# A refitted order of steps, five large probability tiles for four, and other makers of low parts in a hybrid attention layer

## The chip, the cores and the metric

The kernel runs on one core of one Trainium2 chip, all of its work in one launch. The metric is the device time of an execution in microseconds (us). Before the change the median of three timed runs is 360.08 us (359.06 to 360.17). A core has five engines with a queue each, all run in the order in which they were issued: PE (TensorE, with its weight loads as PEld), DVE (VectorE), ACT (ScalarE), POOL (GpSimd) and SP (SyncE, here only DMA issues).

## The reference, cut to what matters

One layer on 512 tokens of width 1024, all in float32:

```python
h = x @ w_in                      # 1024 -> 4114 columns: q, k, v, gates of three mixers
o_nsa = nsa_mixer(...)            # 6 heads: compressed, selected and window attention, gated
o_sb  = stick_breaking_mixer(...) # 4 heads: log_sigmoid scores, reversed cumsum, exp, times v
o_hg  = hgrn2_mixer(...)          # 6 heads: gated linear attention in chunks of 64
mixed = concat([o_nsa * silu(nsa_z), o_sb * silu(sb_z), rms(o_hg) * silu(hg_z)])
x = layer_norm(ALPHA * x + mixed @ w_out, ln_g, ln_b)
```

## The kernel before, in words

Precision first, since it sets the amount of work. A float32 matrix product is made of products of a high and a low part: `hi` is the operand rounded to the narrower type fp32r, `lo` is what is left, and three matmuls (hi with hi, lo with hi, hi with lo) add up in PSUM. So each piece of weights that arrives in a `raw` tile needs two more instructions before PE can use it: the cast to `hi` and the making of `lo`. `load_part` (L277 to L293) does this for 128x1024 elements at a time. The table `SPLITS` says, for each group's first and for its later parts, who makes `lo`: 3 means that ACT casts (L281) and negates (L282), and a DMA of POOL's queue adds the original onto the negation (L284 reads the weights from DRAM again if the group is in `FROM_DRAM`, L286 reads `raw`); 1 means a subtraction on DVE, 0 the same subtraction on POOL (both L293).

The work is cut into named steps. Projections with weights as the moving operand (`blocks`, matmuls L337, 512 columns) are hf1, hq, sq, sk, q, q_kc, vc_ks, kw_sz, sz_nz and nz; with tokens as rows (`tiles`, L353, 256 columns) hi, hi_sv, sv_vs, vw and hz. p0, p1 and p2 are the pairs of heads of the gated linear attention: six times DVE makes a masked query `qz` (L821) and a key `kz` (L796, exponential on ACT), PE multiplies them (L823), DVE copies the product under a mask into `att` (L831); after that come `kt`, the state `st` and the output. s0 to s3 are the stick-breaking heads (scores on PE L385, then ACT and DVE by turns, DVE's running sum L703); v0 to v3 multiply their probabilities with values: `pv` transposes them into `mb` (L403), ACT casts `ph` and DVE makes `pl` (L183, L184), PE adds into the one accumulator `pc` (L410), and `fold` (ACT L140, DVE L425) empties it into `su`. ck and cv are the compressions (L551), c0, c1 and n0 to n11 the scores and probabilities of the first mixer (probabilities in large tiles `pt` of 128x1280 from the pool p5), w0 to w11 their products with values in the way of v0 to v3. f, m, o0, o1 and end finish: `end` multiplies the rest with w_out (L912), adds and normalises.

The order is written out by hand. `ORDER` is a list of step names; a step that has been started is a generator, and each further mention runs it to its next yield. Every mention issues its instructions on all engines at that place; the tile framework then sets each engine's queue from that, with the parts under `high_priority` ahead. So moving a name in `ORDER` moves instructions on PE, DVE, ACT, POOL and SP together. `BUFS` sets the number of buffers of each pool: there is one accumulator (psc=1), so a step v or w can start adding only when the one before has been folded.

Of the kernel before, what the change touches and what calls it, by code (L numbers as in the profile page):

```python
# [38 lines left out]
    hf1=((OFF["hf"] + 256, 128), (OFF["hq"], 128)),  # L39
    hq=((OFF["hq"] + 128, 256),),  # L40
    hi=((OFF["hi"], 256),),
    hi_sv=((OFF["hi"] + 256, 128), (OFF["sv"], 128)),
    sq=((OFF["sq"], 256),),
    sk=((OFF["sk"], 256),),
    sv_vs=((OFF["sv"] + 128, 128), (OFF["vs"], 128)),
    q=((OFF["q"], 64), (OFF["q"] + 192, 64), (OFF["q"] + 64, 64), (OFF["q"] + 256, 64)),
    q_kc=((OFF["q"] + 128, 64), (OFF["q"] + 320, 192)),
    vc_ks=((OFF["vc"], 256),),
    kw_sz=((OFF["kw"], 128), (OFF["sz"], 128)),
    vw_g_hz=((OFF["vw"], 146), (OFF["hz"], 128)),  # L50
    hz=((OFF["hz"] + 128, 256),),
    sz_nz=((OFF["sz"] + 128, 128), (OFF["nz"], 128)),
    nz=((OFF["nz"] + 128, 256),),
)

ORDER = (
# [7 lines left out]
    "end "  # L64
)

BUFS = dict(at=3, g2=31, kkp=4, ma=2, mb=4, nb=3, p0=1, p5=4, psa=3, psc=1, raw=3, sa=8, sb=6, ta=8, tb=10, ti=1,
    w=16)

SPLITS = dict(ck=(1, 1), cv=(1, 1), hf1=(1, 1), hi=(3, 0), hi_sv=(0, 1), hq=(1, 0), hz=(1, 0), kw_sz=(0, 0),  # L70
    nz=(1, 1), o0=(0, 3), o2=(1, 1), o3=(3, 3), sk=(3, 1), sq=(3, 1), sv_vs=(3, 1), sz_nz=(3, 1), vc_ks=(1, 1),
    vw_g_hz=(3, 1))

FROM_DRAM = ('sq', 'sk', 'q', 'q_kc', 'o0', 'o2', 'o4', 'o6')
# [50 lines left out]
class Net:  # L125
# [826 lines left out]
    def body(self, ctx):  # L952
        tc, nc, a = self.tc, self.nc, self.a

        def pool(name, **k):
            n = BUFS.get(name, 1)
            if n:
                k["bufs"] = n
            return ctx.enter_context(tc.tile_pool(name=name, **k))
# [287 lines left out]
```

## Time and profile before

| | |
|---|---|
| median of three runs | 360.08 us |
| profiled execution | 359.79 us |
| its span, first to last instruction | 357.8 us |
| mean granted TensorE clock | 0.994 of full speed |
| busy: PE, DVE, ACT, POOL | 339.3, 291.3, 239.0, 82.4 us |

The span is what the trace shows; 2.0 us of the execution's time lie outside it. A row of the timeline gives the start, the time from there to the end of the last instruction of the row, and in brackets the idle time of the engine ahead of it with what ended that. Busy time is no measure of what bounds the kernel at one place: for that the idle time of PE is looked at stretch by stretch.

### The profile page before, as it was taken

The page shows a single profiled execution, that of the slowest core. Times are in us where ns is not written, and L with a number is a line of the kernel's source. Part 1 is how long each engine was busy: PE and PEld are TensorE (multiplying, and loading weights), DVE is VectorE, ACT ScalarE, POOL GpSimd, SP SyncE. Part 2 cuts the span into 40 slices and gives each one's busy share as a digit, 9 for nine tenths or more (in the row PEclk, how much of TensorE's full clock was granted, in tenths as well). Part 3 has the DMA queues.
Part 4 walks back from the last instruction along what each step waited for, and adds up shares of the span by engine and source line. Part 5 has one row for each costly group of instructions (what it writes and reads, how often), then busy time and mean ns, then how long its engine had stood idle before and what let it go on. Part 6 is the DMA issues. An engine that isn't in the chain of part 4 may idle for free.

```text
span 357.8 us, 5876 instructions
## 1 busy us (share of the span) xinstructions
PE 339.3 (95%) x1994; PEld 288.9 (81%) x1994; DVE 291.3 (81%) x671; ACT 239.0 (67%) x535; POOL 82.4 (23%) x131
## 2 busy tenths in 40 slices
PE   7999999999989989999999999899999999999990
PEld 6778999978778878777887998778888888788880
DVE  4569899889899999987897767668989875769785
ACT  4586772525669997757576666699787874697260
POOL 5063460000400210102400033142021201410074
PEclk9999999999999999999999999999999999999997
DMA  7765547230335564030327847291432180080014
GB/s 267 277 199 159 152 119 236 72 104 2 63 115 117 120 148 87 2 118 2 106 79 203 278 168 205 67 208 34 135 67 52 42 202 23 29 196 12 0 60 176
DMA packets 15909, 42.07 MB, mean 118 GB/s; under 512 B 2626, under 2 KB 3138, under 8 KB 15880
## 3 DMA queue, kind: packets, MB, share of 16 engines
q1 hardware_dynamic: 13432, 33.42, 28.4%
q0 software_dynamic: 2448, 8.29, 13.0%
q8 instruction: 16, 0.26, 0.3%
q14 instruction: 13, 0.11, 0.1%
HBM read 37.06 MB, written 2.12 MB: 110 GB/s over the span
## 4 chain that ended last, share of the span: by engine, by line
PE 62%; DVE 19%; ACT 8%; issue 4%; DMA 3%; POOL 1%; SPq 0%; DVEq 0%; ACTq 0%; POOLq 0%
PE pi L337 20%; PE pi L912 11%; PE pi L353 10%; PE pc L410 6%; PE mb L403 4%; PE ma L385 4%; PE ma L823 3%; DVE sr L703 3%; DMA raw<-w_in 2%; DVE ct L511 2%; DVE qz L821 1%; DVE att L831 1%; DMA xt<-xt 1%; DVE sz L704 1%; POOL ho L447 1%
## 5 line engine op out<-in xcount | busy, mean ns | idle before, releaser
L337 PE MATMUL pi<-xh,hi 128*128 128x512 f32 x160 | 47.4, 406 | 0.1
L337 PE MATMUL pi<-xl,hi 128*128 128x512 f32 x160 | 46.2, 396 | 0.0
L337 PE MATMUL pi<-xh,lo 128*128 128x512 f32 x160 | 46.1, 396 | 0.0
L912 PE MATMUL pi<-hi,mx 128*128 128x512 f32 (+1 forms) x134 | 43.0, 391 | 0.0
L337 PEld LDWEIGHTS pi<-xh,lo 128*128 128x128 f32 x160 | 29.4, 188 | 5.9 <-DVE lo L293 0.4
L337 PEld LDWEIGHTS pi<-xl,hi 128*128 128x128 f32 x160 | 29.5, 188 | 5.7
L337 PEld LDWEIGHTS pi<-xh,hi 128*128 128x128 f32 x160 | 28.5, 188 | 5.5 <-ACT hi L291 0.6
L184 DVE TENSOR_TENSOR pl<-mb,ph 128x384 fp32r<-128x384 f32 (+1 forms) x48 | 27.8, 593 | 3.4 <-ACT ph L183 2.5
L291 ACT CAST hi<-raw 128x1024 fp32r<-128x1024 f32 (+3 forms) x24 | 23.5, 983 | 9.4 <-PE pi L337 4.9
L649 DVE CUSTOM_DVE_ANT_0 pt<-ma,nb 128x256 f32<-128x256 f32 (+3 forms) x42 | 21.3, 513 | 9.5 <-PE ma L385 9.0
L651 ACT ACTIVATE pt<-pt,mn 128x256 f32<-128x256 f32 (+3 forms) x42 | 24.5, 583 | 6.4 <-DVE mn L649 5.9
L183 ACT CAST ph<-mb 128x384 fp32r<-128x384 f32 (+1 forms) x48 | 23.2, 514 | 7.6 <-PE mb L403 7.4
L912 PEld LDWEIGHTS pi<-hi,mx 128*128 128x128 f32 x134 | 24.3, 188 | 4.4 <-PE pi L337 0.4
L353 PE MATMUL pi<-hi,xh 128*128 128x256 f32 (+1 forms) x160 | 27.4, 287 | 0.0
L353 PE MATMUL pi<-hi,xl 128*128 128x256 f32 (+1 forms) x160 | 27.2, 285 | 0.0
L353 PE MATMUL pi<-lo,xh 128*128 128x256 f32 (+1 forms) x160 | 26.7, 285 | 0.0
L912 PE MATMUL pi<-lo,mx 128*128 128x512 f32 (+1 forms) x67 | 26.1, 390 | 0.0
L353 PEld LDWEIGHTS pi<-hi,xh 128*128 128x128 f32 x160 | 23.0, 191 | 0.7
L353 PEld LDWEIGHTS pi<-hi,xl 128*128 128x128 f32 x160 | 22.7, 191 | 0.0
L353 PEld LDWEIGHTS pi<-lo,xh 128*128 128x128 f32 x160 | 22.4, 191 | 0.0
L293 POOL TENSOR_TENSOR lo<-raw,hi 128x1024 fp32r<-128x1024 f32 x7 | 17.7, 2527 | 20.8 <-ACT hi L291 18.9
L293 DVE TENSOR_TENSOR lo<-raw,hi 128x1024 fp32r<-128x1024 f32 (+3 forms) x17 | 19.0, 1117 | 4.2 <-ACT hi L291 2.7
(269 smaller groups left out, 825.9 us busy)
## 6 DMA issues: line engine op xcount, KB each, us to landing
raw<-w_in SPq DMA_DIRECT2D x28, 512.0 KB, 3.7
lo<-w_in POOLq DMA_DIRECT2D x6, 512.0 KB, 5.6
raw<-w_out SPq DMA_DIRECT2D x6, 512.0 KB, 4.1
lo<-w_out POOLq DMA_DIRECT2D x5, 512.0 KB, 7.7
y<-x SPq DMA_DIRECT2D x8, 256.0 KB, 4.3
out<-y SPq DMA_DIRECT2D x8, 256.0 KB, 2.2
xt<-xt SPq DMA_DIRECT2D x3, 512.0 KB, 5.3
nb<-vec SPq DMA_DIRECT2D x6, 256.0 KB, 4.2
```

Source lines behind the costliest of these rows:

```text
L183: nc.scalar.copy(hi, src)
L184: nc.vector.tensor_tensor(out=lo, in0=src, in1=hi.bitcast(F32), op=ALU.subtract)
L291: nc.scalar.copy(hi, raw)
L293: eng.tensor_tensor(out=lo, in0=raw, in1=hi.bitcast(F32), op=ALU.subtract)
L337: self.nc.tensor.matmul(ps, w[:, b * P:(b + 1) * P], self.xpart(x, kt), start=(n == 0 and j == 0), stop=(n == len(grp) - 1 and j == len(js ...
L353: self.nc.tensor.matmul(ps[:, :w_], self.xpart(x, kt)[:, i * P:(i + 1) * P], w[:, :w_], start=(j == 0), stop=(j == len(js) - 1))
L385: self.nc.tensor.matmul(out, lhs, k[e], start=(e == 0), stop=(e == 1))
L403: nc.tensor.transpose(ps[:, o:o + P], pts[i][:, j * P:(j + 1) * P], self.ident)
L410: nc.tensor.matmul(acc[:, j * P:], vt[j], t[:, b:b + w], start=(first and j == 0 and t is h), stop=(last and j == 3 and t is l))
L649: nc.vector.tensor_tensor_reduce(out=dst, in0=src, in1=self.nb[h][:, n - 1::-1], scale=1.0, scalar=3e38, op0=ALU.add, op1=ALU.min, accum_o ...
L651: nc.scalar.activation(dst, dst, AF.Exp, bias=mn, scale=-1.0, accum_out=sm)
L912: nc.tensor.matmul(ps, m, w[:, cs], start=(j == 0), stop=(j == len(jobs) - 1))
```

## The change

Three tables change, no function does. `ORDER` is written anew: the steps are the same ones, as often as before, in places further up or down. The pool p5 has five tiles of 128x1280 in place of four. `SPLITS` changes for three names: sq's first part goes from ACT with a DMA to a subtraction on POOL and its second part from DVE to ACT with a DMA; o0's first half goes from POOL to ACT with a DMA (both halves then are made in that way); o2's first half (128x512) goes from DVE to POOL. The line numbers behind the table are one lower after the change, since `ORDER` has one line less.

```diff
 ORDER = (
-    "x 2*hf1 Lhq hf1 Lhf1 hq Lhi_sv hf1 2*hq hi_sv Lhi hi_sv hq 2*hi_sv 3*p1 hi p1 hi p1 hi p1 hi p0 sk 2*p1 sq 4*p0 "
...
+    "x 2*hf1 Lhq hf1 Lhf1 hq Lhi_sv hf1 2*hq 2*hi_sv Lhi hi_sv hq hi_sv 3*p1 2*hi p1 hi 2*p1 hi p0 sk 2*p1 sq 4*p0 sq "
...
-BUFS = dict(at=3, g2=31, kkp=4, ma=2, mb=4, nb=3, p0=1, p5=4, psa=3, psc=1, raw=3, sa=8, sb=6, ta=8, tb=10, ti=1,
+BUFS = dict(at=3, g2=31, kkp=4, ma=2, mb=4, nb=3, p0=1, p5=5, psa=3, psc=1, raw=3, sa=8, sb=6, ta=8, tb=10, ti=1,
...
-    nz=(1, 1), o0=(0, 3), o2=(1, 1), o3=(3, 3), sk=(3, 1), sq=(3, 1), sv_vs=(3, 1), sz_nz=(3, 1), vc_ks=(1, 1),
+    nz=(1, 1), o0=(3, 3), o2=(0, 1), o3=(3, 3), sk=(3, 1), sq=(0, 3), sv_vs=(3, 1), sz_nz=(3, 1), vc_ks=(1, 1),
```

Three places show what the new order does to the queues. The first is DVE at the sixth of p2's levels, whose two masked queries (one for each head, both into `qz_364`, from `e_1417` before and `e_1431` after) PE needs together; `sz`, `sr` are the stick-breaking heads, `kl` is a key's low part, `att` the masked copy. Before:

```order
L821 TENSOR_TENSOR qz_364<-hq_548,e_1417 64x4x64
L831 COPY_PREDICATED att_1066<-hgmask,ma_1310 128x32x16
...
L703 SCALAR_TENSOR_TENSOR sr_1379<-sr_1379,sl_1378 128x512
L821 TENSOR_TENSOR qz_364<-hq_548,e_1417 64x4x64
L704 TENSOR_TENSOR sz_1093<-sz_1093,sr_1379 128x512
...
L831 COPY_PREDICATED att_1066<-hgmask,ma_1416 128x128x4
L796 TENSOR_TENSOR kz_375<-nk_328,b_326 128x128x3
L821 TENSOR_TENSOR qz_365<-hq_548,e_1444 64x4x64 x2
```

and after:

```order
L820 TENSOR_TENSOR qz_363<-hq_576,e_1390 64x4x64 x2
...
L820 TENSOR_TENSOR qz_364<-hq_576,e_1431 64x4x64 x2
L795 TENSOR_TENSOR kz_375<-nk_328,b_326 128x128x3
...
L696 TENSOR_TENSOR sz_1400<-mb_1512,kept 128x128
L820 TENSOR_TENSOR qz_365<-hq_576,e_1529 64x4x64 x2
```

Both halves of the sixth query now stand together; before, twenty instructions of other steps stood between them. The seventh query (`qz_365` from `e_1444`, after from `e_1529`) stays behind s3's first copies.

The second is PE at ck (L551, after L550) where v2's accumulator (`pc_1890` before, `pc_1859` after) is finished and v0's (`pc_1956`) begun; `pi_2029` is the last projection of vc_ks, `pi_2127` that of kw_sz. Before:

```order
L410 MATMUL pc_1890<-pl_1946,sv_466 128x128
L403 MATMUL mb_2030<-kept,sz_1093 128x128
L337 MATMUL pi_2029<-xh_126,hi_1835 128x512 x2
...
L337 MATMUL pi_2029<-xh_129,lo_1842 128x512 x2
L551 MATMUL pi_2092<-wc_2078,cd_1929 128x256 x3
L410 MATMUL pc_1956<-ph_1962,sv_463 128x512
L551 MATMUL pi_2092<-wc_2078,cd_1929 128x256
```

and after:

```order
L336 MATMUL pi_2017<-xh_129,lo_1842 128x512 x2
L550 MATMUL pi_2092<-wc_2078,cd_1929 128x256 x4
...
L550 MATMUL pi_2092<-wc_2089,cd_1938 128x256 x4
L336 MATMUL pi_2127<-xh_127,hi_2029 128x512
L409 MATMUL pc_1859<-pl_1946,sv_465 128x256
L409 MATMUL pc_1859<-pl_1946,sv_466 128x128
...
L336 MATMUL pi_2127<-xh_128,hi_2035 128x512
L409 MATMUL pc_1956<-ph_1962,sv_463 128x512
```

v0's first accumulating matmul moved from the middle of ck to a place behind all of ck and thirteen matmuls of kw_sz, and v2's last ones moved behind ck as well.

The third is ACT at the gate of nz (`zz_3612` before, `zz_3567` after) and the halves of o0 (`hi_3865` and a later one); `ph` are the casts of w8. Before:

```order
L183 CAST ph_3628<-mb_3623 128x512
L183 CAST ph_3638<-mb_3634 128x384
L291 CAST hi_3521<-raw_3520 128x1024
L291 CAST hi_3865<-raw_3864 128x1024
L430 ACTIVATE zz_3612<-pi_3526 128x512
L281 CAST hi_3871<-raw_3870 128x1024
L431 ACTIVATE zz_3612<-zz_3612 128x512
L282 ACTIVATE lo_3872<-hi_3871 128x1024
```

and after:

```order
L290 CAST hi_3521<-raw_3520 128x1024
L280 CAST hi_3865<-raw_3864 128x1024
L650 ACTIVATE pt_3429,sm_3404<-pt_3429,mn_3403 128x512
L281 ACTIVATE lo_3866<-hi_3865 128x1024
L280 CAST hi_3872<-raw_3871 128x1024
L429 ACTIVATE zz_3567<-pi_3526 128x512
L281 ACTIVATE lo_3873<-hi_3872 128x1024
L430 ACTIVATE zz_3567<-zz_3567 128x512
```

The new negation (`lo_3866`) and the cast of o0's second half now stand ahead of the gate's first step, and w8's two casts stand further down.

## Rows read from the trace of the kernel before

**Rows 1.** The page: busy time of each engine, its share of the span, instructions.

```profile
PE 339.3 (95%) x1994; PEld 288.9 (81%) x1994; DVE 291.3 (81%) x671; ACT 239.0 (67%) x535; POOL 82.4 (23%) x131
```

**Rows 2.** Windows: length, busy PE, PEld, DVE, ACT, POOL, clock, DMA share, GB/s.

```profile
60.00:94.00 34.00, 33.74 (x228) 29.62 (x226) 29.09 (x62) 16.48 (x35) 4.34 (x5) 1.00 0.19 53
94.00:152.00 58.00, 54.19 (x342) 45.97 (x342) 55.50 (x134) 46.82 (x111) 6.87 (x12) 1.00 0.43 101
152.00:190.00 38.00, 36.98 (x195) 29.95 (x194) 32.59 (x58) 24.30 (x43) 7.54 (x7) 1.00 0.28 83
190.00:284.00 94.00, 91.80 (x570) 79.21 (x569) 74.56 (x218) 71.96 (x185) 19.97 (x31) 1.00 0.46 130
284.00:332.00 48.00, 47.94 (x257) 39.74 (x256) 34.79 (x86) 33.95 (x76) 9.00 (x8) 1.00 0.38 94
332.00:357.80 25.80, 16.78 (x83) 13.82 (x81) 18.50 (x38) 8.06 (x17) 11.36 (x9) 0.92 0.22 82
```

**Rows 3.** Waits of PE, whole span: us in total, times, longest.

```profile
PE ma L823 <- DVE qz L821: 2.4, 4, 1.1
PE ma L640 <- DVE pc L637: 1.9, 2, 1.2
PE pc L410 <- DVE su L425: 0.5, 1, 0.5
```

**Rows 4.** Timeline of DVE from 70 to 95 us: start, us, instruction, idle before.

```profile
70.36 0.47 DVE L796 TENSOR_TENSOR kz<-nk,b 128x264 f32<-128x264 f32 x1
70.73 1.22 DVE L293 TENSOR_TENSOR lo<-raw,hi 128x1024 fp32r<-128x1024 f32 x1
73.02 1.30 DVE L831 COPY_PREDICATED att<-hgmask,ma 128x512 f32<-128x512 uint8 x1 [1.06 <-PE ma L823]
...
94.32 1.30 DVE L809 COPY_PREDICATED att<-hgmask,ma 128x512 f32<-128x512 uint8 x1 [1.33 <-PE ma L807]
```

**Rows 5.** Timeline of PE: sq's matmuls with the low parts.

```profile
76.22 1.09 PE L337 MATMUL pi<-xh,lo 128*128 128x512 f32 x4
...
83.38 1.17 PE L337 MATMUL pi<-xh,lo 128*128 128x512 f32 x4
```

**Rows 6.** POOL's subtraction at 44 us, and DVE beside it.

```profile
44.66 2.44 POOL L293 TENSOR_TENSOR lo<-raw,hi 128x1024 fp32r<-128x1024 f32 x1
44.75 2.64 DVE L796 TENSOR_TENSOR kz<-nk,b 128x264 f32<-128x264 f32 x1
```

**Rows 7.** Timeline of DVE: p2's queries of the sixth and seventh level.

```profile
127.42 0.42 DVE L821 TENSOR_TENSOR qz<-hq,e 64x256 f32<-64x256 f32 x1
...
130.22 0.41 DVE L821 TENSOR_TENSOR qz<-hq,e 64x256 f32<-64x256 f32 x1
```

**Rows 8.** Timeline of PE: p2's sixth and seventh level.

```profile
127.90 1.16 PE L823 MATMUL ma<-qz,kz 128*128 128x128 f32 x8 [1.07 <-DVE qz L821]
...
133.55 1.08 PE L337 MATMUL pi<-xl,hi 128*128 128x512 f32 x4
134.47 1.06 PE L823 MATMUL ma<-qz,kz 128*128 128x128 f32 x8
```

**Rows 9.** Timeline of PE at ck.

```profile
182.29 0.51 PE L551 MATMUL pi<-wc,cd 128*128 128x256 f32 x3
183.32 0.47 PE L410 MATMUL pc<-ph,sv 128*128 128x512 f32 x1 [0.53 <-DVE su L425]
```

**Rows 10.** Timeline of DVE at ck.

```profile
182.50 0.68 DVE L425 TENSOR_TENSOR su<-pc,tmp 64x512 f32<-64x512 f32 x1
```

**Rows 11.** Timeline of ACT from 312 to 316 us.

```profile
312.55 0.60 ACT L430 ACTIVATE zz<-pi 128x512 f32<-128x512 f32 x1 [2.33 <-PE pi L337]
313.04 1.04 ACT L281 CAST hi<-raw 128x1024 fp32r<-128x1024 f32 x1
...
314.51 1.05 ACT L282 ACTIVATE lo<-hi 128x1024 fp32r<-128x1024 f32 x1
```

**Rows 12.** Timeline of DVE at the same place.

```profile
319.30 0.68 DVE L453 TENSOR_TENSOR u<-u,zz 128x512 f32<-128x512 f32 x1
```

More of the change, by code (lines that the diff above doesn't have):

```diff
@@ L56 @@
 ORDER = (
[7 rows of a table removed]
-    "end "
[7 rows of a table added]
 )
-BUFS = dict(at=3, g2=31, kkp=4, ma=2, mb=4, nb=3, p0=1, p5=4, psa=3, psc=1, raw=3, sa=8, sb=6, ta=8, tb=10, ti=1,
+BUFS = dict(at=3, g2=31, kkp=4, ma=2, mb=4, nb=3, p0=1, p5=5, psa=3, psc=1, raw=3, sa=8, sb=6, ta=8, tb=10, ti=1,
     w=16)
 SPLITS = dict(ck=(1, 1), cv=(1, 1), hf1=(1, 1), hi=(3, 0), hi_sv=(0, 1), hq=(1, 0), hz=(1, 0), kw_sz=(0, 0),
-    nz=(1, 1), o0=(0, 3), o2=(1, 1), o3=(3, 3), sk=(3, 1), sq=(3, 1), sv_vs=(3, 1), sz_nz=(3, 1), vc_ks=(1, 1),
+    nz=(1, 1), o0=(3, 3), o2=(0, 1), o3=(3, 3), sk=(3, 1), sq=(0, 3), sv_vs=(3, 1), sz_nz=(3, 1), vc_ks=(1, 1),
     vw_g_hz=(3, 1))
```

12 rows, old and new, of the table ORDER are left out of this document.

## The prediction, made before the changed kernel was run

> **What bounds the kernel now.** I read the page first. PE is busy for 339.3 of the 357.8 us of the span [rows 1], 95%; nothing in the change adds or removes a matmul, so all that can be won or lost is PE's idle time, 357.8 - 339.3 = 18.5 us. The second view is the table of windows, which shows where it lies [rows 2]: 332 to 357.8 has 25.8 - 16.78 = 9.02 us (the end, where the other engines normalise), 60 to 94 has 0.26, 94 to 152 has 3.81, 152 to 190 has 1.02, 190 to 284 has 2.20, 284 to 332 has 0.06. These make 16.37; the other 2.1 us lie before 60 us. The third view, the waits of PE, gives names [rows 3]: masked queries `qz` of the gated linear attention 2.4 us in four waits, `pc` of the compressed attention 1.9 in two, the emptying `su` of the accumulator 0.5 in one. Last I looked at DVE in the same windows: from 94 to 152 us it is busy for 55.50 of 58.00 us [rows 2]. There PE and DVE are bounds together, and an order can win at most what DVE itself idles, 2.5 us. Before 94 and between 284 and 332 PE has nothing left to give, so there a change can only cost. The reader is to see that the room of the whole change is 3.81 + 1.02 + 2.20 + 0.26 + 0.06 = 7.35 us, and that by far the most of it lies in three stretches.
>
> **SPLITS of sq: nothing.** The new order takes the 128x1024 subtraction for sq's second part from DVE, 1.22 us [rows 4]. Right behind it DVE waited 1.06 us for a product of PE, and once more 1.33 us at 94.32 [rows 4]: what DVE saves at 71 us lengthens these waits. I count 0; bounds: 0 and a gain of 1.22 - 1.06 = 0.16. The first part's low half is now made on POOL, 2.44 us for this shape [rows 6], in place of a negation and a DMA; PE uses the first part's low half at 76.22 and the second's at 83.38 [rows 5]. The second was ready at 70.73 + 1.22 = 71.95, 11.4 us ahead, so negation and DMA would have to take that much longer than a subtraction to be seen; the first has some six us behind a subtraction that ends near 70. If that cover went, PE would stand at 76.22 or 83.38, in a stretch where its idle time is 0.26.
>
> Here a rule speaks against the change. The trace shows it first: while POOL subtracted at 44.66 for 2.44 us, a key `kz` of DVE beside it took 2.64 us [rows 6], where the same shape takes 0.47 at 70.36 [rows 4]: DVE lost 2.17 us. The Trainium skill (SBUF — State Buffer, section "SBUF: two separate sides") has this as an exclusive lock on a port pair shared by DVE and GpSimd, taken for a whole instruction when a DVE operation has both inputs in SBUF. This trace agrees, by the 2.64. By it sq's new subtraction would cost DVE up to 2.2 us at about 68 to 70 us. By the rows the loss is covered: DVE has 1.22 less to do and waited 1.06 there, 2.28 together. So the term stays 0, and the same mechanism comes back among the rivals at a place without cover.
>
> **SPLITS of o0 and o2.** o0's first half costs ACT a negation more, 1.05 us [rows 11], and POOL a subtraction less. In the new order of ACT this negation and the cast of the second half (1.04, [rows 11]) stand ahead of the gate of nz, where ACT idled 2.33 us [rows 11]: 2.33 - 2.09 = 0.24 to spare. Cost 0, up to 2.1 us if the gate's projection comes sooner. o2's 128x512 subtraction goes from DVE (0.68 for this size, as in [rows 12]) to POOL, half of 2.44 = 1.2 us by estimate. PE has 0.06 us of idle time there [rows 2], so DVE's saving gains nothing: 0.
>
> **Five large tiles.** PE's waits name no large tile that it waits to be given back [rows 3], and between 284 and 332 PE idles 0.06 us [rows 2], so a fifth tile lets instructions be issued further ahead and nothing more by itself: 0, at most those 0.06 us there and the 2.2 - 1.9 = 0.3 of 190 to 284 us that the waits for `pc` leave. The new order uses the room.
>
> **ORDER, 94 to 152 us: a gain of 0.7.** PE waited 1.07 us for the sixth query of p2 [rows 8], whose second half DVE made at 127.42 [rows 7], behind twenty instructions of other steps. In the new order both halves are neighbours, so this wait goes. PE then comes sooner to the seventh level: 1.07 us for the wait, and the projection in between is 8 instead of 20 matmuls of 512 columns, of (134.47 - 133.55) / 4 = 0.23 us each [rows 8], 2.8 us. It would arrive at 134.47 - 1.07 - 2.8 = 130.6. DVE's queries for it stand where they did in its work, from 130.22 on, two of 0.41 [rows 7], and are ready at 131.0. A new wait of 0.4 takes the place of 1.07. The gain is 1.07 - 0.4 = 0.7. Bounds: 0, when DVE's pace alone sets the stretch and each wait comes back elsewhere, and 2.5, DVE's own idle time. The value is nearer to the lower end, since the other waits on queries (2.4 - 1.07 = 1.3 us) have no such change in front of them.
>
> **ORDER, 152 to 190 us: a gain of 0.5.** At 183.32 PE stands 0.53 us in the middle of ck [rows 9], since v0 may not add before `su` has emptied the accumulator, and DVE did that from 182.50 for 0.68 us [rows 10]. Now v0's first matmul comes behind all of ck and thirteen matmuls of kw_sz. v2's last matmuls moved down too, so that `su` has only nine matmuls of 0.23 us, 2.1 us, for its copy on ACT and for its own 0.68 on DVE. That is enough if DVE has no more than about a microsecond in front of it. Bounds: 0 (the wait only moves) and 1.02, PE's whole idle time in the window [rows 2]; I take 0.5, the one wait.
>
> **ORDER, the rest.** 190 to 284 us keep their order but for two scores of the first mixer that change places, and with it the two waits of 1.9 us: 0. From 284 to 332 w8's transposes move behind nz, which can only cost; I take 0. The tail behind the last matmul stays the same.
>
> **Sum.** 0.7 + 0.5 = 1.2 us on the profiled execution of 359.79 us: 358.6. The median of the runs before is 0.29 us above that execution, so I forecast 358.6 + 0.3 = 358.9 us; by itself between 358.2 and 359.8. A measurement of this kernel can tell about 0.3% from no change, 1.1 us: the forecast lies just beyond.
>
> **Rivals.** (a) DVE sets the pace of 94 to 152 us, and the waits only change places. For it: 55.50 of 58.00 busy, and the change takes no DVE work out of that stretch. Against it: the 2.5 us of DVE's idle time. Then only the 0.5 at ck is left, which may move as well: 359.6 to 360.1, no change. Chance 0.25.
>
> (b) The new order closes more: DVE's whole 2.5 us and 0.5 at ck, 360.1 - 3.0 = 357.1. For it: many queue positions moved by several matmuls in just this stretch. Against: the other waits for queries, 1.3 us, keep their causes. Chance 0.13.
>
> (c) POOL's new subtraction for o2 falls on a DVE operation with both inputs in SBUF, such as the `u` at 319.30 [rows 12], and stops DVE for as long as it runs, by the rows of 44 us: up to 1.2 us. The part of the Trainium skill named above would say so of every such meeting. PE has no idle time there, so the casts behind it would show: 358.9 + 1.2 = 360.1, no change. Against: the meeting needs both to start within 1.2 us of each other, and the old subtraction of 2.44 us on POOL some us earlier is gone. Chance 0.12.
>
> (d) Slower: ACT becomes late at nz. The place is the gate's first step; the price is the two instructions put ahead of it, 2.09 us, and it decides from the point where the projection comes more than 0.24 us sooner than ACT is free. Moving w8's work behind nz does bring the projection forward, and the casts of w8 to w11 are queued behind the gate's steps, while PE idles 0.06 us there, so that each late cast shows. With half of the 1.2 us won before it: 360.1 - 0.6 + 2.1 = 361.6. Against: two casts of w8 leave the place ahead of the gate. Chance 0.15.
>
> **How the numbers follow.** The forecast has 0.35: three fifths of it, 0.21, below 359.0 and the rest within 0.3%. (b) adds 0.13 to faster, and (a) 0.05 (the upper end of its room). (a) gives 0.19 to no change, and 0.01 to slower, (c) 0.10 and 0.02, (d) 0.03 and 0.12. This gives faster 0.39, no change 0.46, slower 0.15. The two waits at stake are each some tenths and the new waits are bounds, so I give up some of the middle to both sides: faster 0.43, no change 0.38, slower 0.19. The range for 8 in 10 goes from (b) to a little under (d): 357.1 to 361.4.
>
> **What the profile after would show.** Right: no wait at the sixth level of p2 and one under 0.5 us at the seventh; PE's idle time from 94 to about 151 us near 3.1; no wait for `su` at v0; waits for `pc` at 1.9 still; DVE's wait at 73 us near 1.06 + 1.22 = 2.3 us. Wrong: a PE idle time in the nz stretch of a microsecond or more (d), a DVE subtraction or `u` near 318 us of over 1 us (c), or waits on queries that again add up to 2.4 us (a). Most of all the forecast fails if PE now waits in 94 to 152 us at places that had no wait before.

## The result, and the profile after

The changed kernel takes 356.24 us (median of four, 356.02 to 356.32), the kernel before 360.12 us on the same chip: ratio 0.9898, interval 0.988 to 0.9916. That is faster, by 3.9 us and not by the 1.2 us of the forecast, and 0.9 us below the lower end of the range given. The profiled execution took 356.32 us with a span of 354.1, where before it was 359.79 and 357.8.

The page of the changed kernel, busy time of the engines, against [rows 1]:

```profile
PE 337.3 (95%) x1994; PEld 289.2 (82%) x1994; DVE 290.8 (82%) x669; ACT 240.6 (68%) x536; POOL 84.0 (24%) x133
```

PE ran the same 1994 matmuls in 2.0 us less of busy time. Three windows of the changed kernel, against [rows 2] (length, busy PE, PEld, DVE, ACT, POOL, clock, DMA share, GB/s):

```profile
94.00:152.00 58.00, 54.06 (x343) 46.29 (x343) 55.72 (x134) 46.82 (x110) 6.49 (x12) 1.00 0.42 100
...
190.00:284.00 94.00, 93.39 (x584) 81.21 (x583) 75.81 (x219) 75.19 (x188) 21.05 (x33) 1.00 0.48 131
284.00:332.00 48.00, 47.90 (x255) 39.90 (x254) 35.95 (x85) 33.56 (x76) 7.08 (x8) 1.00 0.38 93
```

The reader is to see that PE's idle time fell where the forecast counted nothing: from 190 to 284 us it went from 2.20 to 0.61 us. From 94 to 152 us it did not fall at all (3.81, now 3.94; near 3.1 was forecast).

Windows of equal clock time hold different work once a kernel runs ahead. So the stages are cut by landmarks as well: PE's first matmul with tokens as rows, the first of ck, the first of cv, the first transpose of f1, the end of the last matmul. Before (length, busy PE, clock, DMA share, GB/s):

```profile
39.56:182.29 142.73, 138.17 (x890) 1.00 0.35 90
182.29:201.67 19.38, 18.82 (x107) 1.00 0.64 191
201.67:239.78 38.11, 36.17 (x260) 1.00 0.62 177
239.78:348.78 109.00, 108.72 (x584) 1.00 0.30 73
```

and after:

```profile
39.57:181.07 141.50, 136.69 (x888) 1.00 0.35 90
181.07:200.48 19.41, 18.95 (x108) 1.00 0.64 184
200.48:237.01 36.53, 36.26 (x260) 1.00 0.66 189
237.01:345.58 108.57, 108.14 (x584) 1.00 0.32 79
```

The span is shorter by 1.23 us up to ck, 1.58 between cv and f1, 0.43 from there to the last matmul and 0.50 behind it; ck itself is the same. The first row holds two small matmuls of v2 less, which now follow ck. Its idle time is 4.81 us after the change and was 4.56 before: what was won there was won in busy time. In [rows 8] four matmuls take 1.08 us, yet their successor starts 0.92 us after their start: a row's modelled end lies 0.16 us beyond the point where PE could go on, and a halt of that length leaves no idle time. So idle time can hide a gain; that such halts are what went here is a reading, and which ones they were is open.

The waits of PE after, against [rows 3] (us in total, times, longest):

```profile
PE ma L822 <- DVE qz L820: 2.0, 3, 0.9
PE mb L384 <- ACT kh L139: 0.7, 1, 0.7
PE pi L550 <- DVE wc L540: 0.5, 1, 0.5
PE ma L639 <- DVE pc L636: 0.3, 1, 0.3
```

The wait for `su` is gone and those for `pc` shrank from 1.9 to 0.3 us. The timeline of PE after, at the places of [rows 8, 9] (start, us, instruction, idle before):

```profile
108.71 2.15 PE L822 MATMUL ma<-qz,kz 128*128 128x128 f32 x16 [0.93 <-DVE qz L820]
...
117.34 1.95 PE L822 MATMUL ma<-qz,kz 128*128 128x128 f32 x16
...
122.35 0.61 PE L384 MATMUL mb<-kh,q 128*128 128x128 f32 x2 [0.68 <-ACT kh L139]
...
130.77 1.13 PE L822 MATMUL ma<-qz,kz 128*128 128x128 f32 x8 [0.93 <-DVE qz L820]
...
183.34 1.35 PE L550 MATMUL pi<-wc,cd 128*128 128x256 f32 x8 [0.46 <-DVE wc L540]
```

### The profile page after: what moved, and what is told of

It is laid out like the page before. It is cut to its first block, busy times and chain, and to the rows that moved or that the text cites. A ratio compares the mean times of both kernels' runs of the same rounds, so it can differ in the third digit from the quotient of the medians.

```text
span 354.1 us, 5843 instructions
## 1 busy us (share of the span) xinstructions
PE 337.3 (95%) x1994; PEld 289.2 (82%) x1994; DVE 290.8 (82%) x669; ACT 240.6 (68%) x536; POOL 84.0 (24%) x133
## 4 chain that ended last, share of the span: by engine, by line
PE 49%; DVE 4%; ACT 2%; issue 1%; POOL 0%; DVEq 0%; ACTq 0%
PE pi L336 14%; PE pi L911 12%; PE pc L409 6%; PE pi L352 5%; PE mb L402 4%; PE ma L384 4%; PE pi L550 1%; PE pc L1143 1%; PE ma L617 1%; DVE q L186 0%; DVE bn L920 0%; PE pi L887 0%; DVE lo L292 0%; DVE sr L702 0%; ACT q L185 0%
## 5 line engine op out<-in xcount | busy, mean ns | idle before, releaser
L911 PE MATMUL pi<-hi,mx 128*128 128x512 f32 (+1 forms) x134 | 44.4, 394 | 0.0
L292 POOL TENSOR_TENSOR lo<-raw,hi 128x1024 fp32r<-128x1024 f32 (+1 forms) x8 | 18.6, 2327 | 36.5 <-ACT hi L290 34.6
L290 ACT CAST hi<-raw 128x1024 fp32r<-128x1024 f32 (+3 forms) x23 | 22.6, 984 | 5.4 <-PE pi L336 2.8
L680 POOL TENSOR_SCALAR pt<-pt,sm,kept 128x512 f32<-128x512 f32 x12 | 10.3, 855 | 50.6 <-DVE sm L677 41.2
```

The lines of the kernel that those rows point to most:

```text
L290: nc.scalar.copy(hi, raw)
L292: eng.tensor_tensor(out=lo, in0=raw, in1=hi.bitcast(F32), op=ALU.subtract)
L911: nc.tensor.matmul(ps, m, w[:, cs], start=(j == 0), stop=(j == len(jobs) - 1))
```

## The experiments

Each ran beside the kernel before on the same chip (359.9 to 360.34 us), and the ratios are to that. The theory after the result was that the fifth large tile, which the prediction had costed at nothing, carries most of the gain; the rival was that the new order does.

**One part at a time, on the kernel before.** The large tiles alone:

```diff
-BUFS = dict(... p5=4, ...)
+BUFS = dict(... p5=5, ...)
```

> The kernel before with five large tiles in place of four, order and SPLITS as before. Theory A (five large tiles change where the framework places the small tiles: the gate tile si gets eight addresses in place of one, so that ACT no longer waits for POOL to give it back, and c1's exponential comes sooner): the wait of 1.2 us for pc L637 at 232 us falls under 0.4, the gate's first step at 229 us is released by PE and no longer by POOL ho, and the time is 358.0 to 358.7. Theory B (the new order makes the whole gain): the waits stay 0.7 and 1.2 and the time stays within 0.5 us of 360.1.

Measured: 358.11 us, 0.9948 (0.9932 to 0.9965), by the ratio 360.3 * 0.0052 = 1.9 us less, as theory A has it. PE waits for no `pc` any more, and the stage from cv to f1 is as short as in the changed kernel although the order is the old one:

```profile
204.04:240.53 36.49, 36.37 (x261) 1.00 0.64 175
```

The order alone:

```diff
-ORDER = (...)   # of before
+ORDER = (...)   # of after
```

> The kernel before with the new order alone, four large tiles and the old SPLITS. Theory A: only the part up to 200 us is won, 0.3 at p1 and 0.9 from 94 to 200 us, so 358.7 to 359.2, and the wait for pc L637 at c1 stays above 1 us. Theory B: 356.2 to 356.8 with no wait for pc L637 above 0.4.

Measured: 360.63 us, 1.0022 (1.0006 to 1.0038), outside the ranges of both theories: the early part's gain does not show in the time. The table SPLITS alone:

```diff
-    o0=(0, 3), o2=(1, 1), sq=(3, 1)
+    o0=(3, 3), o2=(0, 1), sq=(0, 3)
```

> The kernel before with the new SPLITS alone. Both theories: within 0.5 us of 360.1, since what DVE no longer does at 71 us lengthens its wait for PE at 73 us from 1.06 to about 2.3 us. If the subtraction moved to POOL stops DVE, kz at 70 us takes more than 1 us.

Measured: 360.31 us, 1.0003 (0.9992 to 1.0014). So the order by itself wins nothing, SPLITS nothing, and the fifth tile 1.9 us, which leaves some 2 us to parts acting together.

**One part undone, on the kernel after.** Old SPLITS, then four large tiles, then the old order:

```diff
-    o0=(3, 3), o2=(0, 1), sq=(0, 3)
+    o0=(0, 3), o2=(1, 1), sq=(3, 1)
```

> The changed kernel with the old SPLITS, so new order and five large tiles alone. Since the new SPLITS alone moved nothing (360.3 against 360.3): within 0.5 us of 356.2. If the new order needs them: above 357.

Measured: 356.84 us, 0.9909 (0.9893 to 0.9926); the interval overlaps that of the whole change, so SPLITS is worth nothing that can be told, though the median lies 0.1 us outside the range expected.

```diff
-BUFS = dict(... p5=5, ...)
+BUFS = dict(... p5=4, ...)
```

> The changed kernel with four large tiles again: new order and new SPLITS without the fifth tile. If the new order pays only with the fifth tile (it alone took 360.6): 360.0 to 361.0, with waits for pc at c0 and c1 of 0.7 and 1.2 us again and over a microsecond lost at ck and kw_sz. If order and SPLITS pay together without it: below 359.

Measured: 360.54 us, 1.0021 (1.0004 to 1.0038): without the fifth tile the whole gain is gone.

```diff
-ORDER = (...)   # of after
+ORDER = (...)   # of before
```

> The changed kernel with the old order: five large tiles and new SPLITS. As five large tiles alone, since the new SPLITS alone changed nothing: 357.7 to 358.5.

Measured: 358.43 us, 0.9959 (0.9944 to 0.9974). The order is thus worth 358.43 - 356.24 = 2.2 us with five tiles and, by the second experiment, nothing with four. The stages of this kernel differ from those of the changed kernel by the order alone:

```profile
40.36:182.61 142.25, 137.69 (x889) 1.00 0.35 90
182.61:201.94 19.33, 18.95 (x106) 1.00 0.70 212
201.94:238.42 36.48, 36.35 (x260) 1.00 0.62 174
238.42:347.40 108.98, 108.62 (x584) 1.00 0.32 78
```

From the first landmark to the last matmul the new order takes 307.04 - 306.01 = 1.03 us less, with PE busy for 301.62 - 300.04 = 1.58 us less and idle for 0.55 more. This is no matter of one run: up to ck PE is busy for 136.7 to 136.8 us in all six kernels with the new early order, and for 137.7 us or more in all with the old. What four tiles do to the new order is in the windows of PE of the kernel with everything but the fifth one:

```profile
40.25:181.97 141.72, 136.76 (x888) 1.00 0.35 90
181.97:202.47 20.50, 19.34 (x109) 1.00 0.60 177
202.47:240.55 38.08, 36.17 (x261) 1.00 0.64 180
240.55:349.75 109.20, 108.89 (x584) 1.00 0.32 78
```

and in PE's timeline there:

```profile
183.64 0.74 PE L550 MATMUL pi<-wc,cd 128*128 128x256 f32 x4 [0.56 <-DVE wc L540]
...
189.83 0.50 PE L409 MATMUL pc<-pl,sv 128*128 128x512 f32 x1 [0.59 <-DVE pl L183]
...
232.76 0.64 PE L639 MATMUL ma<-kept,pc 128*96 128x128 f32 x4 [1.21 <-DVE pc L636]
```

Up to ck it is as quick as the changed kernel (141.72 against 141.50); between ck and cv it loses 1.09 us, between cv and f1 1.55, then 0.63. The loss between ck and cv can be followed back. PE waits 0.59 us for `pl`, which DVE makes behind `su`, and `su` stands behind a subtraction that took 2.37 us beside two casts of POOL:

```profile
186.24 1.47 POOL L194 CAST kk<-kept 64x512 fp32r<-64x512 f32 x2
```

```profile
186.22 2.37 DVE L292 TENSOR_TENSOR lo<-raw,hi 128x822 fp32r<-128x822 f32 x1
```

In the changed kernel POOL has done these casts long before, and the subtraction takes 1.02 us:

```profile
174.31 1.69 POOL L194 CAST kk<-kept 64x512 fp32r<-64x512 f32 x2
```

```profile
185.36 1.02 DVE L292 TENSOR_TENSOR lo<-raw,hi 128x822 fp32r<-128x822 f32 x1
```

The new order alone, also with four tiles, shows the same meeting (2.37 us at 186.68); the old order with four tiles does not (1.02). The compressions take their `cd` from the pool of the large tiles (L511 before): in the built program the fourth `cd` has the first one's address with four tiles and one of its own with five. That this is why the casts were queued later is not shown.

**Which half of the order.** The new order up to c1 with the old from n0 on, and the other way round, both with five tiles and the new SPLITS:

```diff
 ORDER = (
-    "x ... c0 c1 "      # of before
+    "x ... c0 c1 "      # of after
     "3*n0 ... end "     # of before
```

> The changed kernel (five large tiles, new SPLITS) with the new order up to c1 and the old order from n0 on. If the new order pays where DVE is busy, up to 200 us: 356.0 to 356.7, all of the gain. If it pays in the second half: 357.5 to 358.2, as five large tiles alone.

Measured: 357.11 us, 0.9927 (0.9907 to 0.9947).

```diff
 ORDER = (
     "x ... c0 c1 "      # of before
-    "3*n0 ... end "     # of before
+    "3*n0 ... end "     # of after
```

> The changed kernel (five large tiles, new SPLITS) with the old order up to c1 and the new order from n0 on. If the new order pays up to 200 us: 357.7 to 358.3, as five large tiles alone. If it pays in the second half: 356.0 to 356.7.

Measured: 357.47 us, 0.993 (0.9918 to 0.9943). Both times lie between the ranges expected: neither half has the whole gain. Against the old order in both halves (0.9959) the early half gives 0.0032, the late half 0.0029, and both together 0.0061. So they seem to add up, though each interval is wide (0.9927 and 0.9959 have overlapping ones). In the profiles the early half brings cv forward by 0.6 us (160.97 us behind the first landmark, 161.58 with the old order), less than the 1.3 us of the medians. The late half saves 108.98 - 108.62 = 0.36 us between f1 and the last matmul and some 0.7 behind it.

**Who is waited for between cv and f1.** In the kernel before, a wait for `pc` stands on PE with DVE's name. Behind it, ACT in the kernel before (start, us, instruction, idle before):

```profile
225.80 0.38 ACT L430 ACTIVATE si<-pi 128x256 f32<-128x256 f32 x1 [0.98 <-POOL ho L447]
...
229.50 0.38 ACT L430 ACTIVATE si<-pi 128x256 f32<-128x256 f32 x1 [1.45 <-POOL ho L447]
229.78 0.52 ACT L630 ACTIVATE pc<-pc 128x384 f32<-128x384 f32 x1
```

and in the kernel after:

```profile
226.53 0.38 ACT L429 ACTIVATE si<-pi 128x256 f32<-128x256 f32 x1 [0.84 <-PE pi L352]
226.94 0.53 ACT L629 ACTIVATE pc<-pc 128x384 f32<-128x384 f32 x1
```

Before, ACT's first step of the gate for hz (`times_silu`) could not write `si` until POOL had multiplied the previous one into `ho`. The exponential of `pc` for c1 stood behind it on ACT; DVE's sum came after that, and PE after the sum. After, ACT waits for PE's projection alone. The pool of `si` has one buffer by its table in both kernels, but the tile framework chooses addresses when it builds the program: with four large tiles all eight `si` lie at one address, with five at eight. The theory: it is the address of `si`, not the large tile, that removes these waits. Other pools get new addresses with five tiles as well (`tmp` eight in place of four), so the gate has to be tried by itself. In the changed kernel all gates got one fixed tile; beside it the built program moves only six small tiles (`eb` and five of the compressions):

```diff
-        t = self.tp["ti"].tile([P, 2 * P], F32, tag="ti", name=self.nm("si"))[:, :P * len(us)]
+        t = self.si1[:, :P * len(us)]
```

> The changed kernel with one fixed tile for the gate si of hz and vw, which every use takes, in place of the eight addresses that five large tiles had given it; all else as in the changed kernel. If the gate tile was what five large tiles changed at c0 and c1: the wait for pc at c1 comes back with about 1 us, ACT waits for POOL ho before the gate's first step, and the time is 1.2 to 1.8 us above the changed kernel's 356.2, so 357.4 to 358.0. If the room of other small tiles did it: within 0.4 us of 356.2.

Measured: 358.83 us, 0.9959 (0.9943 to 0.9975), 0.8 us above the range expected. In the profiles the time from the first landmark to the last matmul grows by 307.84 - 306.01 = 1.83 us, as forecast; another 0.78 us lies ahead of the first landmark, where runs vary. PE's waits are back, 0.60 us at c0 and at c1:

```profile
231.50 0.64 PE L639 MATMUL ma<-kept,pc 128*96 128x128 f32 x4 [1.24 <-DVE pc L636]
```

and ACT shows why:

```profile
229.00 0.38 ACT L429 ACTIVATE si<-pi 128x256 f32<-128x256 f32 x1 [1.45 <-POOL ho L446]
```

The stage from cv to f1 is 38.03 us long again; the two stages before it keep what they had won:

```profile
40.35:181.84 141.49, 136.66 (x888) 1.00 0.35 90
181.84:201.26 19.42, 18.94 (x108) 1.00 0.64 188
201.26:239.29 38.03, 36.19 (x261) 1.00 0.62 179
```

The same fixed tile in the kernel before with five large tiles:

```diff
-BUFS = dict(... p5=4, ...)
+BUFS = dict(... p5=5, ...)
-        t = self.tp["ti"].tile([P, 2 * P], F32, tag="ti", name=self.nm("si"))[:, :P * len(us)]
+        t = self.si1[:, :P * len(us)]
```

> The kernel before with five large tiles and one fixed tile for the gate si: old order, old SPLITS. If the gate tile is most of what the fifth large tile gives with the old order: about 1.8 us above five large tiles alone (358.1), so 359.5 to 360.2, with c1's wait of about 1.2 us back. If the fifth tile gives it by itself: 358.1.

Measured: 359.91 us, 0.9998 (0.9985 to 1.0012). With the gate held at one address the fifth tile by itself gives nothing that can be told, and the stage from cv to f1 is 38.04 us again. PE waits for `pc` once more:

```profile
231.89 0.64 PE L640 MATMUL ma<-kept,pc 128*96 128x128 f32 x4 [1.23 <-DVE pc L637]
```

The opposite experiment was to win this without the large tile, by two buffers for the gate in the kernel before:

```diff
-BUFS = dict(... ti=1, ...)
+BUFS = dict(... ti=2, ...)
```

> The kernel before with two buffers of the gate tile si in place of one, nothing else. Theory A, with the gate tile as the whole cause: 358.0 to 358.7, as the one with five large tiles; c1's wait under 0.4 us. If five large tiles act by other tiles that get more addresses: within 0.5 us of 360.1. Theory B: 360.1.

Measured: 361.27 us, 1.0029 (1.0015 to 1.0043), a miss. The change did not do what it was for: in the built program seven of the eight `si` still lie at one address, and only the first gate of hz has another. A wait for `pc` remains on PE:

```profile
224.56 0.61 PE L640 MATMUL ma<-kept,pc 128*96 128x128 f32 x4 [0.96 <-DVE pc L637]
```

The first transpose of f1 comes 197.18 us behind the first landmark, in the kernel before 200.22, but some ten matmuls that stood ahead of it now stand behind. PE's busy time of the stage is 1.80 us less, so only about 1.2 us of the 3.0 are a gain. Behind it more is lost: PE idles 1.62 us up to the last matmul (0.28 before), 0.81 of that for `mx` of ACT. Another small pool has fewer addresses here (sa 10 where it had 13); whether these cause the new waits was not separated. So one more buffer is not one change: it moves others, and this run neither supports the theory of the gate nor speaks against it.

## Why the prediction was wrong

**Five large tiles.** This is the step that failed: "a fifth tile lets instructions be issued further ahead and nothing more by itself: 0". It was argued from PE's waits, which name no large tile. The runs show -1.9 us for it alone (ratio 0.9948) and 356.24 - 360.54 = -4.3 us under the new order. What was waited for was a gate tile of another pool, by ACT, and PE's wait bore the name of DVE, two links further on. With one address for the gate nearly all of the 1.9 us go without the new order (0.9948 to 0.9998, 1.8 us); with it 1.8 us by the stages and 358.83 - 356.24 = 2.6 by the medians. Of the rest of the 4.3, 1.09 us lie between ck and cv, by the trace behind DVE's halt beside POOL's casts; what is left is open.

**"All that can be won or lost is PE's idle time."** This premise failed as well. It holds for the fifth tile: between the two kernels with the old order and the new SPLITS, four tiles and five, the time from the first landmark to the last matmul falls from 308.82 to 307.04 us with PE's busy time the same within 0.1 us. It does not hold for the order, whose 1.03 us came out of busy time while idle time grew.

**"190 to 284 us keep their order ... and with it the two waits of 1.9 us: 0".** The same failure at its place. The stage from cv to f1 got 1.58 us shorter, and its idle time fell by 1.67 (1.94, now 0.27). The order has no part in it, since five tiles with the old order give the same 36.49 us; what the waits hung on changed. They should have been followed back to ACT's `si` and POOL's `ho`, which the trace of before shows.

**ORDER, 94 to 190 us, a gain of 1.2.** Right in direction with five tiles, but forecast at about double its size. The sixth level's wait is gone as forecast; the seventh has 0.93 us and not 0.4, a wait of 0.93 at the second level stays, and s3's `kh` is now 0.68 us late. `su` is no longer waited for, but 0.46 us for `wc` stands in its place, close to the bound "0 (the wait only moves)". With five tiles the new order brings cv forward by 161.58 - 160.97 = 0.6 us. The profiles show 1.20 us between before and after at that landmark, 162.11 - 160.91. The rest is partly the one profiled run of before: PE's busy time up to ck is 138.17 us there and 137.7 to 137.8 in all six other kernels with the old early order. Why that run held 0.4 us more is open. And this gain needs the fifth tile: at four, the stage from ck to cv takes it back (20.50 us against 19.41).

**SPLITS: 0.** Right, by 1.0003 for the table alone. The DVE wait forecast at 2.3 us came to 2.17, on DVE of the changed kernel:

```profile
70.04 0.46 DVE L795 TENSOR_TENSOR kz<-nk,b 128x264 f32<-128x264 f32 x1
72.68 1.31 DVE L830 COPY_PREDICATED att<-hgmask,ma 128x512 f32<-128x512 uint8 x1 [2.17 <-PE ma L822]
```

**The tail "stays the same".** It is 0.5 us shorter, and this size was not forecast at all. All of it lies behind DVE's last instruction. Before:

```profile
352.50 1.40 DVE L941 SCALAR_TENSOR_TENSOR y<-y,rs,mb 128x512 f32<-128x512 f32 x2
```

and after:

```profile
349.30 1.40 DVE L940 SCALAR_TENSOR_TENSOR y<-y,rs,mb 128x512 f32<-128x512 f32 x2
```

From the last matmul to the end of this row it is 353.90 - 348.78 = 5.12 us before and 350.70 - 345.58 = 5.12 after. From there to the end of the span it is 3.9 us before, 3.4 after: the last outputs leave sooner. POOL's nine operations on earlier rows start 7.17 us ahead of PE's end before, 7.64 after:

```profile
341.61 11.59 POOL L948 TENSOR_TENSOR y<-y,ln 128x512 f32<-128x512 f32 x9 [18.26 <-ACT y L943]
```

```profile
337.94 11.60 POOL L947 TENSOR_TENSOR y<-y,ln 128x512 f32<-128x512 f32 x9 [19.19 <-ACT y L942]
```

The tail goes with the late half of the order in every kernel: 8.3 to 8.6 us with the new one, 8.9 to 9.3 with the old. That earlier outputs make room for the last ones is the reading; no run isolates it.

**The rivals.** (b) came nearest in time, 357.1 us, but not in its way: DVE's idle time from 94 to 152 us was not closed. (a) is half right, since the waits there did change places. (c) did not happen. POOL's subtraction for o2 meets a subtraction of DVE only in its last 0.15 us, and neither that one nor the `u` behind it takes longer than usual:

```profile
312.81 1.29 POOL L292 TENSOR_TENSOR lo<-raw,hi 128x512 fp32r<-128x512 f32 x1 [1.83 <-ACT hi L290]
```

```profile
313.95 0.71 DVE L292 TENSOR_TENSOR lo<-raw,hi 128x512 fp32r<-128x512 f32 x1
314.58 0.68 DVE L452 TENSOR_TENSOR u<-u,zz 128x512 f32<-128x512 f32 x1
```

(d) did not happen either: PE idled 0.10 us from 284 to 332. ACT's gate starts right behind the cast put ahead of it (308.25), and 0.4 us after its projection's row ends on PE (307.90):

```profile
308.28 0.60 ACT L429 ACTIVATE zz<-pi 128x512 f32<-128x512 f32 x1
```

## What to carry to other kernels

A wait that a profile names after one engine is to be followed back, engine by engine, until something other than a queue ends it; here PE waited for DVE, DVE for ACT, and ACT for a small buffer that POOL still held. Where a framework places the buffers itself, a number in one pool's table can change other pools too: read the addresses of the built program on both sides before such a change is costed at nothing. And idle time of a pipelined engine is not the whole room: here the order's gain was counted as busy time.

## What the runs showed of the hardware

The halt of DVE beside a subtraction of POOL, 2.64 us for the `kz` of [rows 6], did not come at the two new places: `lo` at 313.95 us starts 0.15 us before the end of POOL's row and takes 0.71, and the `kz` at 70.04 takes 0.46 and starts after sq's new subtraction, on POOL:

```profile
67.33 2.39 POOL L292 TENSOR_TENSOR lo<-raw,hi 128x1024 fp32r<-128x1024 f32 x1 [14.36 <-ACT hi L290]
```

The lock that the Trainium skill describes (SBUF — State Buffer, section "SBUF: two separate sides") is borne out by the 2.64 us; these meetings are too short to test it again.

It did come elsewhere: with four tiles and the new order DVE's subtraction of 128x822 took 2.37 us beside POOL's casts of 1.47 us, 1.02 without them.

The start varies from run to run by more than some parts of the change: the first landmark lies between 39.47 and 42.45 us. In the profiled run with five large tiles alone, which has the 42.45, PE waited 1.80 us at 10.78 for the first inputs, and the clock granted from 10 to 18 us was 0.79 of full speed, where the runs before and after the change have 1.00. Therefore stages were compared from a landmark behind it, and the start was left out.
